# One layer of a hybrid attention and state-space encoder: Strassen products kept for keys, values, queries and gates only

## The chip, the cores and the metric

The kernel runs on one core of a Trainium2 chip. The time is the device time of one execution in microseconds (us). The engines are PE (TensorE: matrix products), DVE (VectorE), ACT (ScalarE), POOL (GpSimd) and SP (SyncE, which issues all the DMAs of this kernel). PEld is the weight load of PE. A product's small operand is called the weights here, the wide one the moving operand.

## The reference

One layer is computed for 2048 prompt frames and 32 sample frames, all in float32. `h` is the normed input, and one wide projection of `h` feeds every branch:

```python
h = RMSNorm_pre(x)                               # (L, 1024)
q, k, v, g_att, z, xbc, dt_raw, gate_a, gate_s = split(h @ w_in)   # 9760 columns
att = window_attention(rope(q), rope(k), v, sinks)                 # 16 heads, 4 of keys
branch_a = (att * silu(g_att)) @ w_attn_o
xs, B, C = split(silu(causal_conv4(xbc)))                          # 2048 + 512 + 512 columns
y = chunked_scan(xs, softplus(dt_raw + dt_bias), B, C) + d_skip * xs   # 32 heads, state 128
branch_s = group_rms_norm(y * silu(z)) @ w_ssm_o
out = (sigmoid(gate_a) * branch_a + sigmoid(gate_s) * branch_s) @ w_out
x = x + RMSNorm_post(out)
```

The outputs are `x` of both groups of frames, the newest keys and values, the conv tails and the final scan states.

## The kernel before

**Blocks and stages.** The prompt is cut into four blocks of 512 frames (blocks 0 to 3, `b` in the code). Block 1 also carries the 32 sample frames, so it has 544 columns. Everything is kept transposed: features on partitions, frames as columns. A block runs through three stages. In the *scan stage* it projects x, B, C and z and runs the chunked scan of four groups beside these products; the first three output products of the scan branch (`ssm_out`, 24 jobs for groups 0 to 2) are in it too. In the *attention stage* it projects keys, values, queries and attention gates, then the merge gates GS and GA; attention runs beside the first of these, and the eight `ssm_out` jobs of group 3 as well. In the *merge stage* it computes the attention output product (`ao`) and the last product (`ou`), beside which the next block's `h` is prepared (`stage_a`).

**Precision.** An operand `x` is split into a high part rounded to fp32r and the remainder, and a product takes three matmuls of such parts (`group`, line 178: 4 contraction tiles by 3 combinations, 12 matmuls). `h` stands in SBUF as `h1` (features 0 to 511) and `h2` (512 to 1023), each with both parts.

**Jobs and weights.** The program is a list of jobs in order (`jobs`). A projection job is a *pair* of 128 output columns. Each needs a list of weight entries of 128 partitions by 512 values; an entry with both parts is 512 KB. An entry is either computed from the raw weights (`alloc`: load 256 KB into `raw`, ACT rounds it at line 142, DVE subtracts at line 143) or loaded as ready parts from DRAM (line 131, `w<-wd`). Where `keep` is set, the computed parts are written to DRAM (line 147, `wd<-w`) for the later blocks. There are nine `w` buffers and four `raw` buffers; `supply` runs eight entries ahead of PE.

**Two ways to compute a pair.** `emit_both` takes the four plain entries a11, a12, a21, a22 and computes the two output tiles one after the other: 48 matmuls of 512 columns. ACT copies each tile out of PSUM (line 247). `emit_pair` computes the same pair by a Strassen step with seven products of half the columns: 84 matmuls of 256 columns (272 in block 1), with weight entries a11, a12, s2, s1, s3, s4, a22 and moving operands b11, b21, t2, t1, t3, b22, t4 (sums of quarters of `h`, made once per block in `stage_a`: `sums_a`, `sums_b`, `sums_c`). Its results are put together by ACT (line 293) after product 0 and by DVE (lines 295, 297, 299, 300) after products 2, 4 and 6; both write into the job's output tile. A Strassen pair uses two PSUM tiles of two banks each, out of two in the pool, so each is awaited again within a pair.

In block 0 every pair is computed by `emit_both`. While that goes on, POOL forms the four weight sums s1, s3, s2, s4 out of the raw entries (line 136), ACT and DVE split them, and five of the eight entries (a11 and the four sums) are written to DRAM. In blocks 1 to 3 every pair is a Strassen pair: 38 of them per block, 20 in the scan stage (8 of x, 4 of B and C, 8 of z) and 18 in the attention stage. Entries a12 and a22 are not all in DRAM: block 1 computes both from raw weights (and writes a12), blocks 2 and 3 load a12 and compute a22.

**What orders the work.** Beside the products, the steps of the scan, the attention and the norms are handed out one at each `tick`: twice per pair and once for every two entries of the other jobs. A scheduler then fixes the order on each engine, and moves matmuls of the next job in front of ones that must wait. Each engine then runs its instructions in that order. SP waits in order too: a DMA whose data or buffer isn't ready holds up those behind it. The small products of the scan (lines 627 to 670: chunk transposes, state and output products) stand in PE's order between the matmuls of line 178. The other lines that the prediction names are L680, where DVE updates the scan state H, L714, where POOL sums squares for the group norm, L1090, where ACT copies the `ou` product out (24 matmuls of 512 columns per job), and L121, the raw load.

## Time and profile before

| what | value |
|---|---|
| device time, three runs | 3401.42 us median (3390.09 to 3412.6) |
| device time of the profiled execution | 3400.23 us |
| its span, first to last instruction | 3398.4 us |
| granted TensorE clock, mean | 0.947 of full speed |
| PE busy | 3010.3 us (89%) |
| PE weight loads busy | 2636.6 us (78%) |
| DVE, ACT, POOL busy | 2283.3 (67%), 1315.1 (39%), 742.0 us (22%) |
| DMA moved | 827.30 MB, mean 243 GB/s |

Busy times are unions over the whole span and hide that the stages differ. Matmuls are pipelined, so their listed durations overlap and a busy PE isn't PE at its peak. The granted clock has two levels, 2.4 GHz (1.0) and 1.2 GHz (0.5); a mean of 0.88 in a stretch says that 24% of it ran at the lower one. The stages end and begin, in us from the span's start: block 0 scan 25 to 545, attention 545 to 885, merge to 1000; block 1 scan 1000 to 1440, attention to 1740, merge to 1855; block 2 scan 1855 to 2253, attention to 2528, merge to 2630; block 3 scan 2630 to 3024, attention to 3296, merge to the end.

### The profile page before, as it was taken

What the parts mean: (1) busy time and instruction counts of PE and PEld (TensorE: products, weight loads), DVE (VectorE), ACT (ScalarE), POOL (GpSimd) and SP (SyncE); (2) the same over time, 40 slices, a digit from 0 to 9 for tenths busy, and PEclk for the clock granted to TensorE, in tenths of its full rate; (3) what the DMA queues carried; (4) which work ended last, traced back from release to release, by engine and by line L of the source; (5) the groups of instructions that cost most, each with busy time, mean ns of one, the idle gap of its engine ahead of it and who ended that gap; (6) DMA issues with size and microseconds to landing.
All of it is one profiled execution on the core that took longest, in us unless ns stands there. A gap on an engine that the chain in (4) does not pass through costs nothing.

```text
span 3398.4 us, 55609 instructions
## 1 busy us (share of the span) xinstructions
PE 3010.3 (89%) x20263; PEld 2636.6 (78%) x20263; DVE 2283.3 (67%) x4427; ACT 1315.1 (39%) x3064; POOL 742.0 (22%) x778
## 2 busy tenths in 40 slices
PE   6878787888898889989999878999999988999998
PEld 5656566656688788988899777888888877888897
DVE  7887977677478868666635766766634877765732
ACT  5555544455344434224413433322413434322411
POOL 2554534233202322110010222120000222210000
PEclk9888888999999999999999988999999998999999
DMA  6667676737888878785786887886686887887684
GB/s 206 225 221 242 210 230 231 248 138 244 288 302 287 267 233 270 224 289 170 227 276 218 281 257 235 284 278 218 200 308 211 289 277 235 274 278 232 191 310 132
DMA packets 511993, 827.30 MB, mean 243 GB/s; under 512 B 38792, under 2 KB 334056, under 8 KB 511720
## 3 DMA queue, kind: packets, MB, share of 16 engines
q1 hardware_dynamic: 511720, 823.75, 73.5%
q8 instruction: 161, 2.64, 0.3%
q14 instruction: 112, 0.92, 0.1%
HBM read 638.50 MB, written 185.12 MB: 242 GB/s over the span
## 4 chain that ended last, share of the span: by engine, by line
PE 54%; DVE 16%; DMA 11%; POOL 6%; issue 6%; ACT 4%; SPq 2%; POOLq 0%; DVEq 0%; ACTq 0%
PE mm L178 45%; POOL raw L136 4%; DVE w L143 3%; DMA rr<-cd 3%; DMA raw<-in_w_in_dram 2%; DMA w<-wd 2%; PE sd L940 1%; DVE u L559 1%; PE sd L983 1%; DMA s<-zd 1%; PE sd L662 1%; PE sd L666 1%; SPq L121 1%; ACT rr L635 1%; DMA s<-rd 1%
## 5 line engine op out<-in xcount | busy, mean ns | idle before, releaser
L178 PE MATMUL mm<-h,w 128*128 128x256 f32 (+2 forms) x7432 | 1308.5, 328 | 206.0 <-ACT w L142 66.7
L178 PEld LDWEIGHTS mm<-h,w 128*128 128x128 f32 x7432 | 1102.1, 197 | 359.3 <-ACT w L142 77.2
L178 PE MATMUL mm<-t,w 128*128 128x256 f32 (+1 forms) x4104 | 574.2, 289 | 2.4 <-DMA w<-wd 2.4
L143 DVE TENSOR_TENSOR w<-raw,w 128x512 fp32r<-128x512 f32 x520 | 441.9, 861 | 160.5 <-ACT w L142 150.2
L178 PEld LDWEIGHTS mm<-t,w 128*128 128x128 f32 x4104 | 534.1, 193 | 8.2 <-issue 4.8
L178 PE MATMUL mm<-v,w 128*128 128x512 f32 (+1 forms) x2400 | 495.4, 360 | 26.6 <-ACT w L142 10.3
L142 ACT ACTIVATE w<-raw 128x512 fp32r<-128x512 f32 x520 | 321.2, 629 | 475.7 <-PE mm L178 203.1
L178 PEld LDWEIGHTS mm<-v,w 128*128 128x128 f32 x2400 | 397.3, 192 | 99.8 <-ACT w L142 12.3
L136 POOL TENSOR_TENSOR raw<-raw 128x512 f32<-128x512 f32 x152 | 228.8, 1505 | 295.0 <-DVE w L143 256.5
L635 ACT ACTIVATE rr<-rr,ncum 128x128 f32<-128x128 f32 (+1 forms) x544 | 167.9, 384 | 110.8 <-POOL rr L632 110.5
L299 DVE TENSOR_TENSOR xq<-mm,xq 128x512 f32<-128x512 f32 (+1 forms) x99 | 69.5, 702 | 167.9 <-PE mm L178 167.7
L178 PE MATMUL mm<-tA,w 128*128 128x512 f32 (+2 forms) x688 | 174.4, 341 | 0.0
L559 DVE SCALAR_TENSOR_TENSOR u<-xq,par,u 128x512 f32<-128x512 f32 x192 | 155.5, 831 | 11.0 <-ACT u L550 8.9
L821 POOL TENSOR_TENSOR s<-s,cs 128x512 f32<-128x512 f32 (+1 forms) x40 | 62.9, 1582 | 438.7 <-DVE s L819 313.5
L921 ACT ACTIVATE pt<-sd,nm 128x192 f32<-128x192 f32 (+3 forms) x260 | 105.0, 413 | 134.3 <-DVE nm L915 131.4
L632 POOL TENSOR_SCALAR_AFFINE_SELECT rr<-rr 128x1024 f32<-128x1024 f32 (+1 forms) x68 | 83.5, 1228 | 259.4 <-DMA rr<-cd 199.3
L178 PEld LDWEIGHTS mm<-tA,w 128*128 128x128 f32 x688 | 118.3, 188 | 13.7 <-ACT v L1090 0.2
L297 DVE TENSOR_TENSOR xq<-mm,xq 128x512 f32<-128x512 f32 (+1 forms) x99 | 69.3, 700 | 75.2 <-PE mm L178 74.4
L295 DVE TENSOR_TENSOR xq<-mm,xq 128x512 f32<-128x512 f32 (+1 forms) x99 | 69.0, 697 | 73.4 <-PE mm L178 72.9
L178 PE MATMUL mm<-S,w 128*128 128x512 f32 (+2 forms) x344 | 115.8, 337 | 0.1
L646 POOL TENSOR_TENSOR s<-xd,te 128x512 f32<-128x512 f32 (+1 forms) x68 | 75.8, 1117 | 172.2 <-DVE xd L643 171.2
L651 POOL TENSOR_TENSOR xl<-s,xh 128x512 fp32r<-128x512 f32 (+1 forms) x68 | 94.5, 1392 | 76.0 <-ACT xh L650 76.0
(272 smaller groups left out, 3990.6 us busy)
## 6 DMA issues: line engine op xcount, KB each, us to landing
w<-wd SPq DMA_DIRECT2D x838, 512.0 KB
wd<-w SPq DMA_DIRECT2D x292, 512.0 KB
raw<-in_w_in_dram SPq DMA_DIRECT2D x306, 256.0 KB
rr<-cd SPq DMA_DIRECT2D x64, 512.0 KB
ee<-cd SPq DMA_DIRECT2D x128, 128.0 KB
x<-in_x_prompt_dram SPq DMA_DIRECT2D x24, 512.0 KB
zd<-xq SPq DMA_DIRECT2D x48, 256.0 KB
s<-zd SPq DMA_DIRECT2D x48, 256.0 KB
```

Source lines behind the costliest of these rows:

```text
L136: pl.tensor_tensor(*(rawtiles[en["raw0"] + i] for i in (dst, x, y)), op=op)
L142: act.activation(w[:, 0], r, AF.Copy)
L143: vec.tensor_tensor(w[:, 1], r, w[:, 0].bitcast(F32), op=ALU.subtract)
L178: last_mm[0] = pe.matmul(ps, a[:, k, :], r(k, n0, n), start=start and k == 0 and i == 0, stop=stop and k == HK - 1 and i == len(ops) - 1)
L297: vec.tensor_tensor(two(y1), m57, twice(y0[:, n:]), op=ALU.add)
L299: vec.tensor_tensor(mid, m34, two(y1), op=ALU.add)
L559: vec.scalar_tensor_tensor(o[:, d0:d0 + n], src[:, t:t + n], convw[:, t, ci:ci + 1], o[:, d0:d0 + n], op0=ALU.mult, op1=ALU.add)
L632: pl.affine_select(w[:q, :, :q], w[:q, :, :q], pattern=[[0, 8], [1, q]], compare_op=ALU.is_ge, fill=-1e30, base=0, channel_multiplier=-1)
L635: act.activation(w[:q, h, :q], w[:q, h, :q], AF.Exp, scale=1.0, bias=ncum[:q, co + g * 8 + h:co + g * 8 + h + 1])
L646: pl.tensor_tensor(xe[:q].rearrange("p (h d) -> p h d", h=8), xd[:q], te[:q, hs].unsqueeze(2).broadcast_to([q, 8, 64]), op=ALU.mult)
L651: pl.tensor_tensor(xl[:q], xe[:q], xh[:q].bitcast(F32), op=ALU.subtract)
L921: act.activation(dst, src, AF.Exp, bias=nm[:, i:i + 1], scale=0.125, accum_out=den[:, i:i + 1])
```

## The change

**Which pairs are Strassen pairs.** `add_pair` gets a flag `fast`, set for keys, values, queries, attention gates, GS and GA (18 pairs per block). The 20 pairs of the scan stage are now computed by `emit_both` in blocks 1 to 3 too, with 48 matmuls of 512 columns (96 of 272 columns in block 1).

**Weights.** In block 0 the 20 plain pairs form no sums and write their four plain entries to DRAM; the 18 fast ones write seven entries (a11, a12, a22 and the four sums). Blocks 1 to 3 compute no entry: four loads for a plain pair, seven for a fast one.

**PSUM in `emit_both`.** For up to 512 columns both output tiles of a pair now share one PSUM tile of two banks; before, each had a tile of its own. In block 1 each has its own tile, split into two banks. ACT still copies each tile out.

**Quarters of `h`.** `h1` and `h2` now hold all four quarters b11, b12, b21, b22 through the scan stage, which the plain products need. t1, which lives where b12 does, is computed in four pieces in `sums_b`, written to DRAM (`t1d`), and brought back by `fetch_t1`, two DMAs put ahead of the last eight `ssm_out` jobs of the scan stage. The job for dt uses the plain form in all blocks (`emit_dt` goes).

```diff
--- before.py
+++ after.py
@@ emit_both @@
         flat, width, off = jb["dest"]()
+        tb = jb["tb"]
+        ts = [banks()] if tb <= 512 else [banks(), banks()]
         for i in range(2):
             if i:
                 between()
-            t = banks()[:, 0]
+            res = [(ts[0][:, i], 0, tb)] if tb <= 512 else [(ts[i][:, x, :n], n0, n) for x, (n0, n) in enumerate(split_n(tb))]
 
             def run():
-                for h, e in enumerate(jb["entries"][2 * i:2 * i + 2]):
...
-                    yield from group(t, e, m, 0, BT, h == 0, h == 1)
-            spread(run(), 6 * HK)
+                for ps, n0, n in res:
+                    for h, e in enumerate(jb["entries"][2 * i:2 * i + 2]):
...
+                        yield from group(ps, e, m, n0, n, h == 0, h == 1)
+            spread(run(), 6 * HK * len(res))
             used(2)
-            y = flat[:, off + i * width:off + i * width + BT]
-            act.copy(y, t)
+            y = flat[:, off + i * width:off + i * width + tb]
+            for ps, n0, n in res:
+                act.copy(y[:, n0:n0 + n], ps)
             jb["evac"][i](y)
@@ add_pair @@
-    def add_pair(b, view, c1, c2, tb, dest, evacs, **kw):
+    def add_pair(b, view, c1, c2, tb, dest, evacs, fast, **kw):
         a11, a12, a21, a22 = ((view, k0, c) for c in (c1, c2) for k0 in (0, HK))
+        kind = "pair" if b and fast else "both"
         if b == 0:
...
-                entries.append(dict(kind="plain", key=(c1, "a11"), load=False, keep=i == 0, raw=r0 + i, free=0))
+                entries.append(dict(kind="plain", key=(c1, name), load=False, keep=not fast or i != 2, raw=r0 + i,
+                                    free=0 if fast else 1))
 
             for name, dst, x, y, op, free in (("s1", 3, 2, 3, ALU.add, 0), ("s3", 2, 0, 2, ALU.subtract, 0),
-                                              ("s2", 0, 3, 0, ALU.subtract, 0), ("s4", 1, 1, 0, ALU.subtract, 4)):
+                                              ("s2", 0, 3, 0, ALU.subtract, 0), ("s4", 1, 1, 0, ALU.subtract, 4)) if fast else ():
...
-            kind = "both"
         else:
-            load = dict(a11=True, a12=b > 1, a22=False)
-            es = [raw_entry((c1, n), u, load.get(n, True), n == "a12" and b == 1)
-                  for n, u in (("a11", a11), ("a12", a12), ("s2", None), ("s1", None), ("s3", None), ("s4", None), ("a22", a22))]
-            kind = "pair"
+            names = ("a11", "a12", "s2", "s1", "s3", "s4", "a22") if fast else ("a11", "a12", "a21", "a22")
+            es = [raw_entry((c1, n), None, True, False) for n in names]
@@ stage_a @@
             def sums_a():
-                parts("b11", "b11")
+                for n in ("b11", "b12", "b22", "b21"):
+                    parts(n, n)
+
+            def sums_b():
+                nh = tb // 2
                 to("b11", "b12", "b11")
                 to("b12", "b22", "b12")
-                parts("t1", "b11")
-
-            def sums_b():
-                parts("b22", "b22")
-                parts("b21", "b21")
                 to("b22", "b22", "b11")
-                parts("t3", "b12")
+                st["t1d"] = dram.tile([P, 2, HK, HN], F32, name="t1d")
+                for k in range(HK):
+                    t = s2.tile([P, 2, HN], F32R, name="s2")
+                    act.activation(t[:, 0, :nh], raw("b11")[:, k], AF.Copy)
+                    vec.tensor_tensor(t[:, 1, :nh], raw("b11")[:, k], t[:, 0, :nh].bitcast(F32), op=ALU.subtract)
+                    dma(st["t1d"][:, :, k, :nh], t[:, :, :nh].bitcast(F32))
 
             def sums_c():
                 to("b21", "b21", "b22")
+                parts("t3", "b12")
@@ the job list @@
+        def fetch_t1(bk=bk, n=tb // 2):
+            for s_ in range(2):
+                dma(operand("t1", n)[:, s_].bitcast(F32), bk["st"]["t1d"][:, s_, :, :n])
...
         ssm_out(2)
+        if b:
+            jobs[-8]["pre"].append(fetch_t1)
...
-            (emit_dt if j else emit_plain)(j)
+            emit_plain(j)
```

**On PE, scan stage of block 3.** Before, the second pair of x and the first product of the third pair: `mm` are PSUM tiles, `h1`, `h2`, `t2` to `t4` the moving operands, `w` the weight buffers; after each row stands what it waits for (Activation and DVE: those engines, DMAHW: a DMA).

```order
L178 MATMUL mm_26637<-h1_99,w_26380 128x256 x2
L178 MATMUL mm_26637<-h2_100,w_26455 128x256 [waits DMAHW7_49,Activation_49]
L178 MATMUL mm_26637<-h2_100,w_26455 128x256 x11
L178 MATMUL mm_26637<-t2_101,w_26479 128x256 [waits DMAHW0_49]
L178 MATMUL mm_26637<-t2_101,w_26479 128x256 x11
L178 MATMUL mm_26638<-h1_99,w_26493 128x256 [waits DMAHW1_49,DVE_49,PE_49]
L178 MATMUL mm_26638<-h1_99,w_26493 128x256 x11
L178 MATMUL mm_26638<-t3_102,w_26545 128x256 [waits DMAHW4_49]
L178 MATMUL mm_26638<-t3_102,w_26545 128x256 x11
L178 MATMUL mm_26766<-h1_99,w_26598 128x256 [waits DMAHW7_49,DVE_49]
L178 MATMUL mm_26766<-h1_99,w_26598 128x256 x11
L178 MATMUL mm_26638<-h2_100,w_26559 128x256 [waits DMAHW5_49,DVE_49]
```

The same stage of the changed program, the third pair and the first product of the fourth:

```order
L178 MATMUL mm_24919<-h1_99,w_24642 128x512 [waits DMAHW4_49]
L178 MATMUL mm_24919<-h1_99,w_24642 128x512 x11
L178 MATMUL mm_24919<-h2_100,w_24644 128x512 [waits DMAHW5_49]
L178 MATMUL mm_24919<-h2_100,w_24644 128x512 x11
L178 MATMUL mm_24999<-h1_99,w_24806 128x512 [waits DMAHW2_49,Activation_49]
L178 MATMUL mm_24999<-h1_99,w_24806 128x512 x3
L178 MATMUL mm_24919<-h1_99,w_24720 128x512 [waits DMAHW0_49,Activation_49]
L178 MATMUL mm_24919<-h1_99,w_24720 128x512 x11
L178 MATMUL mm_24919<-h2_100,w_24722 128x512 [waits DMAHW1_49]
L178 MATMUL mm_24919<-h2_100,w_24722 128x512 x11
L178 MATMUL mm_24999<-h1_99,w_24806 128x512 x8
L178 MATMUL mm_24999<-h2_100,w_24808 128x512 [waits DMAHW3_49]
```

Before, the tile `mm_26637` waits for ACT after its first product (`h1_99`, then `h2_100`) and the second tile `mm_26638` for DVE ahead of its third; the next pair's `mm_26766` is begun early, and waits for DVE. Now one tile, `mm_24919`, takes both halves of a pair, and the second half (`w_24720`) waits for ACT; three or four matmuls of the next pair's tile `mm_24999` stand ahead of it.

**On SP, scan stage of block 0.** Before (`wd<-w`: ready parts to DRAM; `raw`: raw weights; `zd`: the z gate to DRAM):

```order
L147 DMA wd30_718<-w_714 128x1024
L147 DMA wd31_724<-w_720 128x1024
L147 DMA wd32_730<-w_726 128x1024
L147 DMA wd33_736<-w_732 128x1024
L121 DMA raw_738<-in_w_in_dram 128x4x128
L121 DMA raw_740<-in_w_in_dram 128x4x128
L121 DMA raw_742<-in_w_in_dram 128x4x128
L121 DMA raw_744<-in_w_in_dram 128x4x128
L577 DMA zd_795<-xq_757 128x512
L147 DMA wd34_786<-w_783 128x1024
L577 DMA zd_795<-xq_757 128x512
L147 DMA wd38_865<-w_861 128x1024
```

And now, at the same group's z pairs:

```order
L147 DMA wd18_639<-w_636 128x1024
L121 DMA raw_641<-in_w_in_dram 128x4x128
L147 DMA wd19_646<-w_643 128x1024
L121 DMA raw_648<-in_w_in_dram 128x4x128
L147 DMA wd20_688<-w_685 128x1024
L121 DMA raw_690<-in_w_in_dram 128x4x128
L147 DMA wd21_695<-w_692 128x1024
L121 DMA raw_697<-in_w_in_dram 128x4x128
L147 DMA wd22_739<-w_736 128x1024
L121 DMA raw_741<-in_w_in_dram 128x4x128
L147 DMA wd23_746<-w_743 128x1024
L121 DMA raw_748<-in_w_in_dram 128x4x128
```

Before, four raw loads follow a run of four writes, the last of which waits for the pair's last sum. Now each write is followed by one raw load, four entries ahead.

## Rows read from the trace of the kernel before

**Rows 1.** windows of the stages: us; then each engine's busy us (instructions), PEclk, DMA share, GB/s

```profile
25.00:545.00 520.00, 415.98 (x1898) 324.61 (x1896) 425.98 (x603) 257.84 (x516) 230.76 (x195) 0.88 0.68 227
545.00:885.00 340.00, 284.60 (x1368) 208.51 (x1368) 240.67 (x453) 173.82 (x408) 120.58 (x84) 0.92 0.60 210
1000.00:1440.00 440.00, 383.97 (x2987) 364.50 (x2986) 339.14 (x687) 172.70 (x404) 115.54 (x188) 0.94 0.81 259
1740.00:1855.00 115.00, 114.72 (x923) 114.14 (x922) 45.81 (x113) 31.70 (x64) 11.16 (x10) 1.00 0.65 213
1855.00:2253.00 398.00, 346.54 (x2519) 316.82 (x2518) 293.04 (x552) 146.59 (x331) 84.76 (x108) 0.94 0.82 266
2494.60:2527.00 32.40, 31.22 (x248) 30.20 (x249) 8.81 (x14) 5.25 (x11) 0.19 (x1) 1.00 0.92 325
2630.00:3024.00 394.00, 351.39 (x2540) 319.78 (x2539) 294.67 (x541) 146.58 (x332) 83.29 (x106) 0.95 0.81 269
900.00:950.00 50.00, 50.00 (x226) 40.61 (x225) 27.30 (x59) 20.10 (x37) 12.37 (x10) 1.00 0.97 321
```

**Rows 2.** waits of PE, scan stage of block 0: us in total, times, longest

```profile
PE mm L178 <- ACT w L142: 39.4, 13, 6.8
PE sd L662 <- DVE H L680: 19.5, 6, 6.4
PE sd L733 <- POOL s L714: 15.1, 3, 7.3
PE mm L178 <- DVE w L143: 9.3, 9, 2.3
```

**Rows 3.** waits of PE, scan stage of block 1

```profile
PE mm L178 <- DVE xq L295: 20.1, 4, 12.0
PE mm L178 <- DVE xq L299: 18.7, 15, 3.8
```

**Rows 4.** waits of PE, scan stage of block 2

```profile
PE mm L178 <- ACT xq L293: 11.8, 6, 6.9
PE mm L178 <- DVE xq L295: 10.7, 5, 8.7
...
PE mm L178 <- DVE xq L297: 4.9, 5, 2.4
PE mm L178 <- DMA w<-wd: 3.7, 3, 1.6
```

**Rows 5.** waits of PE, scan stage of block 3

```profile
PE mm L178 <- DVE xq L297: 7.0, 5, 5.3
...
PE mm L178 <- ACT xq L293: 5.2, 6, 2.2
PE mm L178 <- DVE xq L295: 4.4, 4, 1.9
```

**Rows 6.** groups by line, whole span: count, busy us, mean ns, idle before

```profile
L143 DVE TENSOR_TENSOR w<-raw,w 128x512 fp32r<-128x512 f32 x520 | 441.9, 861 | 160.5 <-ACT w L142 150.2 <-PE mm L178 2.5 <-DMA raw<-in_w_in_dram 0.6
```

**Rows 7.** timeline of evacuations, quiet stretches of block 2: start us, us, instruction

```profile
2505.37 0.42 DVE L300 TENSOR_TENSOR xq<-mm,xq 128x256 f32<-128x256 f32 x1
2516.21 0.42 DVE L300 TENSOR_TENSOR xq<-mm,xq 128x256 f32<-128x256 f32 x1
...
2612.08 0.59 ACT L1090 COPY v<-mm 128x512 f32<-128x512 f32 x1 [4.93 <-PE mm L178]
2617.60 0.59 ACT L1090 COPY v<-mm 128x512 f32<-128x512 f32 x1 [4.93 <-PE mm L178]
```

**Rows 8.** timeline of PE in the same quiet stretch

```profile
2496.28 1.57 PE L178 MATMUL mm<-t,w 128*128 128x256 f32 x12
2497.69 1.59 PE L178 MATMUL mm<-h,w 128*128 128x256 f32 x12
```

**Rows 9.** timeline of POOL and DVE, attention stage of block 0

```profile
828.82 6.04 POOL L136 TENSOR_TENSOR raw<-raw 128x512 f32<-128x512 f32 x4 [11.84 <-DVE w L143]
...
830.79 1.22 DVE L143 TENSOR_TENSOR w<-raw,w 128x512 fp32r<-128x512 f32 x1 [2.10 <-ACT w L142]
...
835.57 0.69 DVE L143 TENSOR_TENSOR w<-raw,w 128x512 fp32r<-128x512 f32 x1
```

More of the change, by code (lines that the diff above doesn't have):

```diff
@@ L1247, in qjobs @@
             c = C_Q + kv * 256
[L1248 removed]
+            pair(c, c + P, bk["stage_dest"], [bk["evac_q"](kv, a) for a in range(2)], name=("q", b, kv), fast=True)
         def gjobs(kv, **kw):
             c = C_G + kv * 256
[L1252 removed]
+            pair(c, c + P, bk["g_dest"](kv, ph), [bk["silu2"]] * 2, name=("g", b, kv), fast=True, **kw)
             if kv >= 2:
```

33 lines of the change are left out of this document (9 added, 24 removed).

## The prediction

> **What bounds the kernel now.** I read the windows of the stages first, because the change touches the three kinds of stage differently. In a quiet stretch of the gates GS and GA (2494.6 to 2527) PE is busy 31.2 of 32.4 us at full clock [rows 1]: PE is the bound. The scan stages are different. There PE is idle 104, 56, 51.5 and 42.6 us in blocks 0 to 3 (window less PE's busy time), and the granted clock is 0.88, 0.94, 0.94 and 0.95 [rows 1], so 24%, 12%, 12% and 10% of the time ran at 1.2 GHz. Then I read PE's waits in each scan stage, to see who ends the idle time. In block 0 it is mostly the weights: 39.4 + 9.3 = 48.7 us until a split entry is there (lines 142, 143), and 34.6 us of the scan's own waits for DVE and POOL [rows 2]. In blocks 1 to 3 the largest waits are for the evacuations of Strassen pairs: 38.8 us in block 1 [rows 3], 27.4 us in block 2 [rows 4], 16.6 us in block 3 [rows 5]. DVE, which makes most of these evacuations, is busy 82%, 77%, 74% and 75% of the four scan stages (426 of 520, and so on) [rows 1]. So the scan stages are bound by PE and DVE together: each waits for the other in turn.
>
> **What a pair costs on PE.** In the quiet stretch a Strassen pair ends every 10.84 us, and two `ou` jobs, which have the 48 matmuls of 512 columns of a plain pair, take 2 x 5.52 = 11.04 us [rows 7]. Seven products alone would take 7 x 1.41 = 9.9 us [rows 8]; the other 0.9 us of a quiet Strassen pair are its own waits. So the Strassen step saves 1.1 us of PE work per pair and gives 0.9 us back in its waits even where nothing else runs. For block 1 a matmul of 272 columns takes 115 / 923 = 0.125 us [rows 1], so a plain pair there is 96 x 0.125 = 12.0 us against 84 x 0.125 = 10.5 us: 1.5 us more.
>
> **Block 0, scan stage: -100 us.** Removed: for 20 pairs four sums on POOL, four splits each on ACT and DVE, and one write of 512 KB per pair. A split costs DVE 0.861 us on average [rows 6], so DVE loses 80 x 0.861 = 69 of its 426 us. PE's matmuls stay the same. What goes: the 48.7 us of waits for weights, since eight entries ahead are now two pairs instead of one and a raw load no longer waits for the pair's sums; about half of the 34.6 us of scan waits, because DVE and POOL have room, 17 us; and clock: at block 2's 0.94 the stage would run about 50 us at the lower level instead of 125, and with PE 80% busy that gives back 75 x 0.8 / 2 = 30 us. Sum 96. A second way: block 2's scan stage does the same scan beside the same pairs in 398 us; add about 20 us for DVE's remaining 104 splits and it is near 415, 105 us less than 520. I take 100. The bounds are 49 (only the weight waits) and 135 (down to 385 us, PE's 416 busy us less the 30 of the clock).
> The remaining splits should also get shorter. While POOL forms sums, a split takes 1.22 us on DVE, and 0.69 us when POOL has ended [rows 9]. The Trainium skill, "SBUF — State Buffer", section "SBUF: two separate sides", says that VectorE with two SBUF inputs and GpSimd take a shared port pair in turn, each for a whole instruction. The trace agrees, by that difference. By that rule the 104 splits left would cost 0.69 instead of 0.861 us, 18 us less of DVE's time; I don't add it to the sum, since PE waits for DVE only at times.
>
> **Block 0, attention stage: +8 us.** The work of 18 fast pairs stays, with two more writes each: 36 x 512 KB = 18.9 MB on top of 210 GB/s x 340 us = 71 MB [rows 1], which makes 266 GB/s, under the 321 GB/s that the windows show elsewhere. They are issued while POOL forms sums and few transfers are under way. Also the second half of each pair now waits for the ACT copy of the first with nothing in between. Bounds: nothing, and 36 x 1.63 = 59 us if every write at 321 GB/s stood in the path.
>
> **Block 1, scan stage: -20 us.** Twenty pairs at 1.5 us more PE work add 30 us. The evacuation waits of 38.8 us go: each half has its own PSUM tile, and before that tile is used again a whole half (6 us) runs. Their share of the lower clock goes too: of 12% of 440 us, 53 us, I take half, 26 us, which at PE's 87% gives 11 us. Sum 30 - 39 - 11 = -20. Bounds: +30 if the waits only change place, -40 if the clock goes up fully.
>
> **Blocks 2 and 3, scan stages: -3 and +7 us.** The pairs add 20 x 1.1 = 22 us each. The waits of 27.4 and 16.6 us go, and clock worth 5 us in each. A new wait comes: the second half of a plain pair needs the tile whose first half ACT is still reading. Three or four matmuls of the next pair stand in front, about 0.9 us, where the copy takes 0.59 us (like L1090 [rows 7]). Behind a waiting half stand all of PE's later products and the scan's. If ACT is on time this costs nothing; Strassen's own wait for ACT cost 11.8 us in block 2 [rows 4] with a like cover, so I take 8 us per block. Sums: 22 - 27 + 8 - 5 = -2, written as -3 with the conversions that no longer hold up loads, and 22 - 17 + 8 - 5 = +8, written as +7 for the same reason. Bounds from -30 (no waits left at all) to +21 in each.
>
> **Everything else: +1 us.** Blocks 1 to 3 compute no weights: 152 splits go, and their raw loads on SP's queue. PE's waits for loaded weights, 3.7 us in block 2 [rows 4], should fall by some 5 us in all. Against it, a fast pair now loads 7 x 524 = 3670 KB in 10.84 us, 339 GB/s, where the quiet stretch moves 325 GB/s at a DMA share of 0.92 [rows 1]. If 339 couldn't be had, the pair would take 11.3 us (3670 KB at 325 GB/s), 0.45 us more for some 42 pairs outside the attention steps: 19 us. I take 6, since at 0.92 of the engines there is room. Parking t1 adds per block four small splits, four writes and two reads: in the merge stage ACT idles 4.93 us per `ou` job [rows 7], and the reads have eight `ssm_out` jobs of 2.8 us (half an `ou` job) before the first fast pair. The reads wait on SP for the last z pair's matmuls, as the weight loads behind them do anyway. Cost nothing; if it weren't covered, some 3 us per block.
>
> **Sum.** -100 + 8 - 20 - 3 + 7 + 1 = -107 on the profiled execution's 3400.2 us (span 3398.4 and 1.8 around it), 3293 us. That execution lies 1.2 us under the median of the runs, 3401.4, so I predict 3293 us.
>
> **Rivals.**
> *The waits were all that held the scan stages (3201 us).* Block 0 gains its 135; blocks 1 to 3 lose all idle time and pay the pairs: 30 - 56, 22 - 51.5, 22 - 42.6. With +8 and +6 elsewhere: -213 + 14 = -199, and 3201. For it: DVE loses its splits and all evacuations of the scan stages in blocks 1 to 3. Against it: part of the idle time belongs to the scan's chain, which stays.
> *The copy wait takes Strassen's place (3397 us).* If each of the 60 plain pairs of blocks 0, 2 and 3 waits 2.0 us for ACT (11.8 us in 6 waits [rows 4]), that is 120 us, of which 16 are counted: +104 on the forecast, 3397, about no change. For it: ACT takes its instructions in order, and the scan's exponentials wait there for other engines. Against it: ACT is busy only 37% in block 2. The Trainium skill, "TensorE: Matmul & The Clock Gate", table at its head, says that ScalarE's queue is strictly first in, first out; one Strassen wait for ACT lasted 6.9 us [rows 4], ten times a copy, which agrees.
> *The scan's chain sets the pace (3438 us, slower).* Place: the small scan products in PE's order in blocks 1 to 3. If they wait as long for DVE, POOL and DMAs as before, a removed evacuation wait comes back there, and only the work counts: +30 + 22 + 22. Block 0 then gains only its 48.7, and the +8 and +6 stay: +39. It decides when less than 40 us of all relief beyond the weight waits comes. Against it: the evacuation waits are the largest single waits in blocks 1 to 3.
> *DMA binds (3357 us).* The 59 us of writes in block 0's attention stage and 19 us of loads, less the 14 counted: +64, and 3357. For it: the share of 0.92 in the quiet stretch. Against it: 0.97 and 321 GB/s were borne in block 0's merge stage with PE busy throughout [rows 1].
> *It doesn't do what it says.* The changed order shows 288 splits, all in block 0, and 72 sums: it does.
>
> **How the numbers follow.** Chances: the forecast 0.66, all waits gone 0.12, the copy wait 0.09, the chain 0.05, DMA 0.08. The forecast's own range is 3215 to 3355. The range that holds the time 8 times in 10 reaches from 3210 into the DMA case and short of the copy wait: 3210 to 3365. A measurement of this kernel can tell about 1%, 34 us, from no change. Faster by more than that: forecast, all waits gone and DMA, 0.86. Within it: the copy wait, 0.09. Slower: the chain, 0.05.
>
> **What would show it.** Right: block 0's scan stage near 420 us, with hardly a wait of PE for lines 142 and 143 and a clock of 0.93 or more; block 1's near 420 without waits for DVE on the pairs; blocks 2 and 3 within 10 us of before, with PE waiting for the pair's ACT copy some 8 us in each; the quiet fast pairs at 10.8 to 11.0 us; block 0's attention stage at 340 to 360 us. Wrong: block 0's scan stage above 470, or scan stages of blocks 1 to 3 longer than before.

## The result, and the profile after

The changed kernel takes 3210.7 us (median of four runs, 3203.3 to 3226.0) beside 3396.5 us for the kernel before (median of four too): a ratio of 0.945, 95% interval 0.940 to 0.950. That is 186 us faster. The profiled execution is the slowest of the four (3226.0 us, span 3224.2), so the stages below show 174 us of it. Measured again beside the runs below, the changed kernel took 3220.2 us, ratio 0.949 (0.946 to 0.952).

The gain by stage, from marks that both kernels have: the start of a block's first `s<-mm,dtb`, the end of its first `kr<-mm` (scan stage), the end of its last `tA<-xq` (attention stage), the next block's first mark (merge stage).

| us | scan 0 | attention 0 | merge 0 | scan 1 | attention 1 | scan 2 | attention 2 | scan 3 | attention 3 |
|---|---|---|---|---|---|---|---|---|---|
| before | 510.7 | 346.2 | 105.1 | 450.6 | 299.3 | 409.1 | 274.0 | 403.5 | 271.1 |
| after | 381.5 | 373.6 | 98.3 | 423.8 | 301.3 | 388.4 | 270.3 | 388.7 | 271.2 |
| difference | -129 | +27 | -7 | -27 | +2 | -21 | -4 | -15 | 0 |

The merge stages of blocks 1 to 3 differ by 1 us or less. Each stage is read from one profiled execution. Between executions of the changed kernel and its near copies below, a stage that is the same in both differs by up to 7 us.

From the page of the changed kernel, the engines' busy times and the clock by slices, and the lines of the splits and sums:

```profile
PE 3009.6 (93%) x19007; PEld 2570.8 (80%) x19007; DVE 1935.7 (60%) x3965; ACT 1227.0 (38%) x2942; POOL 617.3 (19%) x698
...
PEclk9999988898999999999999999999999999999999
...
L143 DVE TENSOR_TENSOR w<-raw,w 128x512 fp32r<-128x512 f32 x288 | 238.0, 841 | 96.6 <-ACT w L142 91.9
...
L136 POOL TENSOR_TENSOR raw<-raw 128x512 f32<-128x512 f32 x72 | 104.3, 1448 | 199.7 <-DVE w L143 195.6
```

PE is busy as long as before (3010 us), in a shorter span: the plain pairs of blocks 1 to 3 stream more columns, at a higher mean clock (0.973 of full speed, 0.947 before). The splits fell from 520 to 288 [rows 6], as the changed order showed. The clock is at 9 nearly throughout; the weak slices lie in block 0's attention stage.

The windows of the changed stages: scan 0, attention 0, scan 1, scan 2, scan 3 (columns as in [rows 1]):

```profile
29.00:410.00 381.00, 366.08 (x1868) 292.31 (x1866) 310.31 (x519) 206.24 (x435) 104.75 (x114) 0.99 0.86 283
411.00:784.00 373.00, 304.23 (x1382) 222.87 (x1380) 231.60 (x450) 168.31 (x405) 118.64 (x84) 0.89 0.66 238
883.00:1306.00 423.00, 405.53 (x3300) 391.39 (x3299) 276.27 (x591) 173.27 (x438) 109.72 (x186) 0.98 0.68 206
1711.00:2099.00 388.00, 367.14 (x1886) 295.75 (x1884) 244.06 (x478) 155.66 (x344) 86.56 (x106) 0.98 0.70 215
2463.00:2851.00 388.00, 367.62 (x1891) 295.77 (x1890) 241.47 (x462) 156.07 (x342) 88.06 (x105) 0.98 0.69 213
```

Where PE was idle 104, 56, 51.5 and 42.6 us in the four scan stages [rows 1], it is now idle 15, 17, 21 and 20 us, and the clock rose to 0.98 or 0.99 in each. Only block 0's attention stage went the other way: 69 us idle at a clock of 0.89, where [rows 1] show 55 us at 0.92.

PE's waits (us in total, times, longest) in scan 0; this answers to [rows 2]:

```profile
PE sd L726 <- POOL s L707: 6.5, 3, 2.2
PE mm L178 <- ACT xq L251: 2.8, 3, 1.3
...
PE sd L655 <- DVE H L673: 0.9, 2, 0.6
```

No wait for a weight is left, and the scan's own two largest waits fell from 19.5 + 15.1 to 0.9 + 6.5 us. The view of the kernel before goes on below the four lines of [rows 2] with five more waits of the scan, 17.9 us in all, among them:

```profile
PE sd L631 <- DVE ee L673: 8.7, 2, 4.4
PE sd L631 <- DVE rr L652: 5.1, 1, 5.1
```

So the scan's own waits were 52.5 us, not 34.6. In attention 0 of the changed kernel:

```profile
PE mm L178 <- ACT xq L251: 27.2, 10, 5.5
PE mm L178 <- ACT w L142: 18.1, 12, 2.3
PE mm L178 <- DVE w L143: 5.4, 2, 2.7
```

In scan 1 PE waits 0.5 us for a pair's evacuation instead of 38.8 [rows 3]. In scan 2, then in scan 3, the largest wait is the new one for the ACT copy, where [rows 4, 5] show waits for Strassen's evacuations:

```profile
PE mm L178 <- ACT xq L251: 15.6, 8, 3.9
...
PE mm L178 <- ACT xq L251: 9.2, 6, 2.6
```

A quiet Strassen pair still ends every 10.8 us, as in [rows 7] (10.84):

```profile
2335.84 0.42 DVE L289 TENSOR_TENSOR xq<-mm,xq 128x256 f32<-128x256 f32 x1
2346.63 0.43 DVE L289 TENSOR_TENSOR xq<-mm,xq 128x256 f32<-128x256 f32 x1
```

It now loads seven operands in that time, 3670 KB, or 340 GB/s, without a loss. The trace agrees: from 2325 to 2369 the DMAs moved 341 GB/s at a share of 0.95.

### The profile page after: what moved, and what is told of

Read it like the earlier page. It is cut to its first block, busy times and chain, and to the rows that moved or that the text cites. A ratio compares the mean times of both kernels' runs of the same rounds, so it can differ in the third digit from the quotient of the medians.

```text
span 3224.2 us, 51384 instructions
## 1 busy us (share of the span) xinstructions
PE 3009.6 (93%) x19007; PEld 2570.8 (80%) x19007; DVE 1935.7 (60%) x3965; ACT 1227.0 (38%) x2942; POOL 617.3 (19%) x698
## 4 chain that ended last, share of the span: by engine, by line
PE 61%; DVE 12%; DMA 10%; ACT 6%; POOL 5%; issue 5%; SPq 1%; DVEq 0%; POOLq 0%; ACTq 0%
PE mm L178 51%; DMA rr<-cd 4%; POOL raw L136 2%; ACT rr L628 2%; DVE u L552 2%; DVE w L143 2%; DMA raw<-in_w_in_dram 2%; PE sd L933 1%; PE sd L659 1%; POOL rr L625 1%; PE sd L976 1%; PE sd L655 1%; PE sd L959 1%; DMA s<-zd 1%; PE sd L663 1%
## 5 line engine op out<-in xcount | busy, mean ns | idle before, releaser
L178 PE MATMUL mm<-h,w 128*128 128x512 f32 (+2 forms) x8336 | 1602.4, 346 | 104.7 <-ACT xq L251 54.6
L178 PEld LDWEIGHTS mm<-h,w 128*128 128x128 f32 x8336 | 1317.3, 193 | 324.4 <-ACT xq L251 69.3
L143 DVE TENSOR_TENSOR w<-raw,w 128x512 fp32r<-128x512 f32 x288 | 238.0, 841 | 96.6 <-ACT w L142 91.9
L178 PE MATMUL mm<-t,w 128*128 128x256 f32 (+1 forms) x1944 | 271.2, 287 | 0.0
L178 PEld LDWEIGHTS mm<-t,w 128*128 128x128 f32 x1944 | 249.2, 190 | 4.4 <-issue 4.3
L142 ACT ACTIVATE w<-raw 128x512 fp32r<-128x512 f32 x288 | 174.6, 627 | 157.8 <-POOL raw L136 79.6
L628 ACT ACTIVATE rr<-rr,ncum 128x128 f32<-128x128 f32 (+1 forms) x544 | 168.7, 385 | 131.7 <-POOL rr L625 131.7
L251 ACT COPY xq<-mm 128x512 f32<-128x512 f32 (+1 forms) x226 | 110.9, 508 | 232.1 <-PE mm L178 231.8
L136 POOL TENSOR_TENSOR raw<-raw 128x512 f32<-128x512 f32 x72 | 104.3, 1448 | 199.7 <-DVE w L143 195.6
L906 DVE TENSOR_REDUCE mx<-sd 128x2 f32<-128x384 f32 (+3 forms) x140 | 66.0, 510 | 82.9 <-PE sd L933 78.2
L645 DVE SCALAR_TENSOR_TENSOR rr<-rr,sd 128x1024 f32<-128x1024 f32 (+1 forms) x68 | 79.3, 1165 | 53.0 <-ACT rr L628 53.0
```

Source lines behind the costliest of these rows:

```text
L136: pl.tensor_tensor(*(rawtiles[en["raw0"] + i] for i in (dst, x, y)), op=op)
L142: act.activation(w[:, 0], r, AF.Copy)
L143: vec.tensor_tensor(w[:, 1], r, w[:, 0].bitcast(F32), op=ALU.subtract)
L178: last_mm[0] = pe.matmul(ps, a[:, k, :], r(k, n0, n), start=start and k == 0 and i == 0, stop=stop and k == HK - 1 and i == len(ops) - 1)
L251: act.copy(y[:, n0:n0 + n], ps)
L628: act.activation(w[:q, h, :q], w[:q, h, :q], AF.Exp, scale=1.0, bias=ncum[:q, co + g * 8 + h:co + g * 8 + h + 1])
```

## The experiments

Three things were open: why block 0's attention stage lost 27 us, why scan 0 gained more than forecast, and which part of the change helped blocks 1 to 3. All stage lengths are between the marks above.

### Block 0's attention stage: own tile, or fewer writes

The second half of a plain pair waits for the copy of the first. The timeline of PE and ACT around one such wait in the changed kernel (start us, us, engine, line):

```profile
689.80 4.81 PE L178 MATMUL mm<-h,w 128*128 128x512 f32 x20
698.29 7.39 PE L178 MATMUL mm<-h,w 128*128 128x512 f32 x24 [3.69 <-ACT xq L251]
...
691.89 0.64 ACT L142 ACTIVATE w<-raw 128x512 fp32r<-128x512 f32 x1 [1.71 <-POOL raw L136]
693.26 0.63 ACT L142 ACTIVATE w<-raw 128x512 fp32r<-128x512 f32 x1 [0.74 <-POOL raw L136]
694.95 0.63 ACT L142 ACTIVATE w<-raw 128x512 fp32r<-128x512 f32 x1 [1.06 <-POOL raw L136]
696.62 0.63 ACT L142 ACTIVATE w<-raw 128x512 fp32r<-128x512 f32 x1 [1.04 <-POOL raw L136]
697.16 0.61 ACT L774 ACTIVATE xq<-xq 128x512 f32<-128x512 f32 x1
697.68 0.56 ACT L251 COPY xq<-mm 128x512 f32<-128x512 f32 x1
```

PE ends the first half at 694.61. The copy stands on ACT behind four splits of weight sums, each waiting about 1 us for POOL's next sum, and one short activation, and starts at 697.68. PE goes on at 698.29, right after the copy's end at 698.24. The copy itself is short; what is queued in front of it on ACT is long.

The Trainium skill, "Perfetto Trace Analysis", section "Matmuls", advises to rotate independent groups of matmuls through different PSUM banks, so that the evacuation of one overlaps the next. The two halves here do go to different 512-value slices of the tile, and yet the trace shows the wait. The next run takes it away by giving each half a tile of its own: in this program it goes with the tile, not with the slice.

**A tile for each half** (the edit in `emit_both`, up to 512 columns):

```diff
-        ts = [banks()] if tb <= 512 else [banks(), banks()]
+        ts = [] if tb <= 512 else [banks(), banks()]
...
-            res = [(ts[0][:, i], 0, tb)] if tb <= 512 else [(ts[i][:, x, :n], n0, n) for x, (n0, n) in enumerate(split_n(tb))]
+            res = [(banks()[:, 0, :tb], 0, tb)] if tb <= 512 else [(ts[i][:, x, :n], n0, n) for x, (n0, n) in enumerate(split_n(tb))]
```

> The changed kernel, but each half of a plain pair has its own PSUM tile in blocks 0, 2 and 3 too (they shared one), and nothing else differs. In the changed kernel PE waits for the ACT copy of a plain pair 26.5 us in block 0's attention stage, 15.6 us in block 2's scan stage and 9.2 us in block 3's. Theory A, the shared tile is what cost block 0's attention stage its 27 us: that stage falls from 374 to about 350 us between the markers (first K evacuation to the last product of the attention), the scan stages of blocks 2 and 3 by 5 to 15 us each, and the time goes from 3211 to about 3165 to 3185 us. Theory B, the attention stage is longer because of the two extra writes per fast pair and the sums on POOL: the copy waits vanish but PE waits for weights instead, the stage stays at 365 to 375 us, and the time is 3190 to 3215 us.

Measured: 3167.8 us, ratio 0.934 (0.932 to 0.936). Attention 0 falls to 332.5 us, by 41, more than theory A asked for; scan 2 falls by 16 and scan 3 by 3 us, where 5 to 15 were expected in each. Attention 0 in the window, and PE's largest waits there:

```profile
406.00:738.00 332.00, 285.63 (x1364) 211.58 (x1362) 236.24 (x450) 170.32 (x403) 116.38 (x82) 0.92 0.72 260
```

```profile
PE mm L178 <- ACT w L142: 23.8, 8, 5.5
PE sd L959 <- ACT pt L914: 8.3, 3, 5.5
```

The 27.2 us of copy waits are gone and the weight waits grew only from 18.1 to 23.8 us. PE's idle time fell by 22 us (69 to 46), and its busy time by 19 us (304 to 286) at a higher clock (0.89 to 0.92). Theory A holds: the shared tile cost this stage more than the 27 us. With own tiles the stage is 14 us shorter than before the change; PE waits 26.7 us for weights there, before it was 32.5 + 3.3 = 35.8. Why is not shown.

**Two operands less to write.** For the fast pairs a12 is made again in block 1 and a22 in blocks 1 to 3:

```diff
-                entries.append(dict(kind="plain", key=(c1, name), load=False, keep=not fast or i != 2, raw=r0 + i,
+                entries.append(dict(kind="plain", key=(c1, name), load=False, keep=not fast or i == 0, raw=r0 + i,
...
-            es = [raw_entry((c1, n), None, True, False) for n in names]
+            load = dict(a12=b > 1, a22=False) if fast else {}
+            es = [raw_entry((c1, n), dict(a12=a12, a22=a22).get(n), load.get(n, True), fast and n == "a12" and b == 1)
+                  for n in names]
```

> The changed kernel, but for the fast pairs a12 is made a second time in block 1 and a22 in blocks 1 to 3 from the raw weights, as in the kernel before; so block 0 writes five operands per fast pair instead of seven (less 18.9 MB), and blocks 1 to 3 convert 18 + 54 operands again. Theory A (the shared PSUM tile cost block 0's attention stage its 27 us): that stage falls by less than 8 us from 374, and the conversions in blocks 1 to 3 cost 0 to 15 us in all, so 3205 to 3225 us. Theory B (the extra writes cost it): the stage falls by 15 to 30 us to 345 to 360 us, and the time is 3185 to 3205 us.

Measured: 3217.1 us, ratio 0.948 (0.946 to 0.951). Attention 0 is 371.1 us, 2 us less, within the spread; the copy waits of PE there are 31.4 us. Theory B falls: the 36 writes cost this stage nothing that can be measured, and ready operands for these pairs gain nothing that can be measured on the whole.

### Is the Strassen step worth anything beside the attention

**All 38 pairs plain**, in all blocks; the weight sums, the input's sums and the parking of t1 are gone:

```diff
-            return steps + [[sums_a], [sums_b], [sums_c]]
+            return steps + [[sums_a]]
...
-        pair(C_K, C_K + P, bk["k_dest"], [bk["evac_k"](j) for j in range(2)], need=[f"s{b}.3"], fast=True,
+        pair(C_K, C_K + P, bk["k_dest"], [bk["evac_k"](j) for j in range(2)], need=[f"s{b}.3"],
...
```

> The changed kernel with plain products for all 38 pairs in every block: no Strassen step at all, so no sums on POOL for the weights, none of the input's sums, nothing parked; each weight written once and loaded ready. It asks what the Strassen step beside the attention is still worth. By the quiet rows a plain pair costs PE 0.2 us more than a fast one in blocks 0, 2 and 3 (11.04 against 10.84 us) and about 1.5 us more in block 1: 18 x (3 x 0.2 + 1.5) = 38 us more if only PE's work counts. Theory A (the sums on POOL and the weight waits set block 0's attention stage, with PE busy 293 of 361 us there): that stage falls from 374 by 40 to 70 us, and with the 38 us the time is 3170 to 3215 us. Theory B (the attention's own chain sets that stage): it falls by less than 15 us, and the time is 3230 to 3260 us.

> As the run with all 38 pairs plain, and each half of a pair with its own PSUM tile in blocks 0, 2 and 3. If the copy wait of the shared tile costs PE time (theory A of the first run), this is 30 to 60 us below the all-plain kernel with shared tiles, about 3130 to 3170 us, since all pairs gain. If the copy waits only stand where another wait would stand (theory B), the two agree within 15 us.

Measured: 3114.5 us, ratio 0.918 (0.916 to 0.920), with shared tiles, and 3082.3 us, ratio 0.909 (0.907 to 0.910), with a tile for each half. Both beat the changed kernel, by 3 and 4%. The first lies below even theory A's 3170: attention 0 fell by 104 us, to 269.2, where 40 to 70 were expected. The own tile took another 32 us, at the low end of what was expected (the time itself lies below the 3130 to 3170 us expected, since the kernel with shared tiles already did). Attention 0 gains only 3.5 us of them (269.2 to 265.7): without sums in ACT's queue the shared tile costs this stage almost nothing, with them it cost 41. Of the second kernel, PE's total from the page, and the windows of scan 0 and attention 0:

```profile
PE 2994.2 (97%) x17927; PEld 2515.1 (82%) x17927; DVE 1682.0 (55%) x3644; ACT 1220.0 (40%) x2939; POOL 506.9 (16%) x626
```

```profile
29.00:403.00 374.00, 360.69 (x1857) 290.28 (x1856) 304.69 (x518) 205.35 (x433) 93.03 (x108) 1.00 0.89 292
404.00:669.00 265.00, 264.20 (x1395) 202.59 (x1394) 159.42 (x389) 131.70 (x345) 20.21 (x18) 1.00 0.75 246
```

PE is busy 264.2 of 265 us in attention 0, at full clock. And the price expected for the plain pairs, 38 us, doesn't appear: attention 1, 2 and 3 take 294.3, 266.6 and 266.8 us beside 301.3, 270.3 and 271.2 with Strassen pairs. PE's whole busy time is lower (2994 against 3010 us, at a higher clock), though a plain pair streams 48 x 512 columns and a Strassen pair 84 x 256, an eighth less. In attention 1, 2 and 3 the step does save PE work: PE is busy 281.4, 258.9 and 259.4 us with Strassen pairs and 292.9, 266.0 and 266.2 us without. But PE is idle there 20.0, 11.3 and 11.8 us with them, and 1.5, 0.6 and 0.6 without. So the step saves 7 to 11 us per stage and its waits cost 11 to 19: no stage gets shorter by it. And in block 0 the sums for it cost 67 us more (332.5 against 265.7, own tiles both).

### Why scan 0 gained 129 us: the sums' load, or their chain

Two runs added to that fastest kernel what the sums load on the engines: 152 additions on POOL, then also a copy on ACT and a subtraction on DVE for each, over tiles that nobody else uses. The additions:

```diff
...
+        if en.get("junk"):
+            j = junk["t2"]
+            pl.tensor_tensor(j[1], j[0].bitcast(F32), j[0].bitcast(F32), op=ALU.add)
...
```

> The kernel with all 38 pairs plain and own tiles, plus, for each of the 152 weight operands of block 0, one addition on POOL of the size of a weight sum, over two tiles that nothing else touches: POOL's load of the kernel before, without anyone waiting for its result. It asks whether POOL's time for the sums alone (80 x 1.45 us in the scan stage, 72 x 1.45 in the attention stage) costs something, by the shared port or by the scan's own POOL work queued behind. Theory A (the load on POOL and DVE is what the sums cost): block 0's scan stage goes from 375 us up by 40 us or more and its attention stage from 258 us by 30 or more, splits on DVE get longer towards 0.86 us. Theory B (the chain costs it: a raw buffer comes free only after the sums, and the split of a sum waits for POOL): both stages grow by less than 15 us. Time by A 3150 us or more, by B 3080 to 3110 us.

> As the run with the 152 unread additions, plus for each of them one ACT copy and one DVE subtraction of the size of a split, also over tiles that nothing else touches: the whole engine load of the sums of the kernel before, on POOL, ACT and DVE, without its dependencies and its writes. DVE gets 80 x 0.8 = 64 us more in block 0's scan stage and 58 us more in its attention stage. Theory A (engine load): the scan stage goes from 375 us to above 450 (before: 511) and the attention stage from 258 to above 310 (with the sums: 332). Theory B (the chain of raw buffer, sum, split): the scan stage stays below 420 and the attention stage below 290.

Measured: 3193.9 us (scan 0 470.0 us, attention 0 265.8) and 3236.3 us (495.2 and 267.5). Without them attention 0 is 265.7 us, not 258. By the numbers theory A holds in scan 0 and theory B in attention 0, but the timeline of POOL forbids to read it so:

```profile
122.02 12.20 POOL L153 TENSOR_TENSOR t<-t 128x512 fp32r<-128x512 f32 x11
...
167.50 27.57 POOL L153 TENSOR_TENSOR t<-t 128x512 fp32r<-128x512 f32 x22
```

An instruction that waits for nothing was put early in its engine's order. All additions had run by 206 us (not 170, as the next expectation has it), in rows of up to 22, with the scan's POOL work behind them, and three single waits of PE (29.6, 22.6 and 19.4 us) make most of the loss. Attention 0 had none of the load. The runs say nothing on sums spread over the stages.

So the additions were made to read the raw buffer of each operand, which puts them where it lands (the last two lines in the second run alone):

```diff
...
+            v = r.rearrange("p (k c) -> p k c", k=2)
+            pl.tensor_tensor(j[0], v, v, op=ALU.add)
...
+            act.activation(j[1], j[0].bitcast(F32), AF.Copy)
+            vec.tensor_tensor(junk["t3"][0], j[0].bitcast(F32), j[1].bitcast(F32), op=ALU.subtract)
...
```

> The two runs before this left the question open: an addition that reads nothing of the program stands at the head of POOL's order, and all 152 ran in the first 170 us, in rows of up to 22, so their load wasn't that of the sums. Here the kernel with all 38 pairs plain and own tiles has, for each of the 152 weight operands of block 0, one addition on POOL of the size of a weight sum that reads the raw buffer of that operand, so that it stands where that buffer has landed; nobody reads its result, but the raw buffer comes free only after it. Theory A (POOL's and DVE's load from the sums set block 0's scan stage before): the scan stage goes from 375 us to above 420, with DVE's splits near 0.95 us as before. Theory B (the chain raw, sum, split, buffer free set it): it stays under 395 us. In the attention stage (266 us without sums, 332 with them and own tiles) the load is 72 additions of 1.45 us; A expects above 290 us, B under 275. Time by A 3140 us or more, by B 3080 to 3110 us.

> As the run with additions that read the raw buffers, plus an ACT copy and a DVE subtraction of each addition's result, over spare tiles that PE never reads: sums and splits of the kernel before with the order of that chain, but no PE product waits for them and they are not written. If the sums' whole engine load in its order is what cost block 0's scan stage 511 us (before) against 375, this stage goes above 470 us; if PE's waits for the pair's own weights (a lookahead of one pair) made it, it stays below 430 us. Attention stage: with the sums and own tiles it is 332 us; load alone would give above 310, the chain through PE and the writes below 290.

Measured: 3132.6 us, ratio 0.923 (0.921 to 0.925), and 3178.2 us, ratio 0.936 (0.934 to 0.938). Windows of scan 0 and attention 0, of the run with additions and then, in the second fence, of the one with splits too:

```profile
30.00:439.00 409.00, 372.45 (x1864) 298.93 (x1862) 348.36 (x520) 206.17 (x434) 199.32 (x194) 0.97 0.82 267
439.00:715.00 276.00, 268.84 (x1392) 205.22 (x1391) 186.05 (x389) 132.27 (x345) 93.26 (x79) 0.98 0.72 237
```

```profile
32.00:471.00 439.00, 381.08 (x1855) 302.32 (x1853) 407.89 (x604) 253.51 (x520) 222.27 (x195) 0.94 0.77 249
471.00:762.00 291.00, 276.41 (x1402) 209.77 (x1403) 224.38 (x452) 163.90 (x405) 96.94 (x78) 0.96 0.67 223
```

| us | no sums | + additions | + splits | sums that are used |
|---|---|---|---|---|
| scan 0 | 374.7 | 409.3 | 439.2 | 510.7 (before) |
| attention 0 | 265.7 | 276.4 | 290.8 | 332.5 (changed kernel, own tiles) |

Neither theory holds alone: in both runs both stages lie between the bounds set. In scan 0 the additions cost 35 us and the splits 30, in attention 0 11 and 14. PE's waits in scan 0 of the second run show how, the largest two and the only one for a weight:

```profile
PE sd L715 <- POOL s L696: 16.8, 3, 9.5
PE sd L644 <- DVE H L662: 11.5, 7, 3.9
...
PE mm L185 <- ACT w L143: 1.7, 1, 1.7
```

All waits other than for weights come to 55 us there, where they were 52.5 us in the kernel before and are 13 us without sums. So the load alone, on POOL, ACT and DVE, brings the scan's waits back in full. The last 72 us of scan 0 come only when the sums are part of the program; then PE waits 48.7 us for weights too [rows 2]. The window of the kernel before, between the marks:

```profile
29.00:539.00 510.00, 408.74 (x1868) 319.14 (x1867) 419.88 (x593) 254.04 (x509) 225.09 (x189) 0.88 0.69 228
```

Beside the second run that is 43 us more idle time (101 against 58), about the weight waits, and 28 us more busy time (409 against 381), at a clock of 0.88 instead of 0.94. Three things can make the weights late: raw buffers held through all four sums, a lookahead of one pair, one more entry to write per pair. How the waits divide among them wasn't tried. In attention 0 the last step is 42 us.

### Blocks 1 to 3: plain products, or ready operands

**Strassen with ready operands**: the kernel before, with all seven operands of each pair written in block 0.

```diff
-                entries.append(dict(kind="plain", key=(c1, "a11"), load=False, keep=i == 0, raw=r0 + i, free=0))
+                entries.append(dict(kind="plain", key=(c1, name), load=False, keep=i != 2, raw=r0 + i, free=0))
...
```

> The kernel before, with the Strassen step on all pairs and the sums for all pairs in block 0, but with all seven weight operands of every pair written in block 0 and loaded ready in blocks 1 to 3: nothing but the ready operands of the change. It separates the change's two parts in blocks 1 to 3, whose scan stages fell by 27, 21 and 15 us. Theory A, the plain products beside the scan gave that (no evacuations of Strassen pairs on DVE): here the three scan stages stay within 8 us of before (451, 409, 404 us), and PE still waits for DVE and ACT on the pairs there. Theory B, the removed conversions gave it (38 ACT copies and 38 DVE subtractions less per block after the first): the three stages fall by 40 us or more in all. Block 0 has 76 writes of 512 KB more; by the run that took back 36 writes (the same time, 3217 against 3211 us) that should cost under 15 us. Time by A 3385 to 3405 us, by B 3330 to 3360 us.

**Plain products without ready operands**: the changed kernel, whose plain pairs make a12 again in block 1 and a22 in blocks 1 to 3.

```diff
...
-            es = [raw_entry((c1, n), None, True, False) for n in names]
+            load = {} if fast else dict(a12=b > 1, a22=False)
+            es = [raw_entry((c1, n), dict(a12=a12, a22=a22).get(n), load.get(n, True), not fast and n == "a12" and b == 1)
+                  for n in names]
```

> The changed kernel, but the plain pairs beside the scan make two of their four operands again from the raw weights as the kernel before did (the second of the first half in block 1, the second of the second half in blocks 1 to 3): plain products without the ready operands. It is the complement of the Strassen run with ready operands, which shortened the three scan stages by 10, 17 and 4 us where the whole change shortened them by 27, 21 and 15. If the two parts add, the three stages here are 434, 405 and 393 us (the change's 424, 388 and 389 plus what the ready operands gave). If either part is enough, because both only make room on DVE, they stay within 6 us of the changed kernel's, 418 to 430, 382 to 394 and 383 to 395 us, and the time is 3205 to 3230 us.

| us | scan 1 | scan 2 | scan 3 | ratio to before |
|---|---|---|---|---|
| before | 450.6 | 409.1 | 403.5 | 1 |
| ready operands alone | 440.6 | 392.2 | 399.2 | 0.994 (0.992 to 0.997) |
| plain products alone | 436.9 | 387.4 | 388.9 | 0.956 (0.954 to 0.959) |
| both | 423.8 | 388.4 | 388.7 | 0.945 (0.940 to 0.950) |

The first run fits neither of its theories: 31 us in all, where A allowed 8 per stage and B asked for 40, and a time of 3378.6 us, between the two. Its 76 more writes go with a block 0 that is 19 us longer (scan 0 523.2 us, attention 0 352.5), where under 15 were expected. In scan 1 the two parts seem to add (10 + 14 = 24 of 27 us); with up to 7 us of spread in each stage this is weak. In scans 2 and 3 the plain products alone do all of it. With them PE waits less for DVE anyway, and the ready operands have nothing left to give that these runs show. The second run took 3242.9 us, 13 us above the upper end of what was expected. Its scan 0 is 388.8 us, 7 to 12 longer than in two executions of the changed kernel, although it writes less there; why stays open.

The changed kernel itself, run again beside these:

> The changed kernel again, on the chip of this group, so that the others can be held against it: 3200 to 3220 us, and block 0's attention stage at 370 to 376 us.

Measured: 3220.2 us, 0.2 over what was expected, attention 0 at 371.2 us; the other stages within 5 us of the table at the head.

## Why the prediction was right or wrong

The forecast was 3293 us, the time is 3210.7: the direction is right, and so are the waits that were to go, but the gain is 186 us instead of 107. The time lies 0.7 us inside the stated range (3210 to 3365) and below the forecast's own (3215 to 3355), and two of the four executions lie below both. That it is inside is luck: had block 0's attention stage lost the 8 us that were forecast and not 27, the time would be some 19 us less. What was wrong is the sentence "part of the idle time belongs to the scan's chain, which stays": of 104, 56, 51.5 and 42.6 us idle in the scan stages, 15 to 21 are left. The rival "The waits were all that held the scan stages", with a chance of 0.12, describes these stages better (3201 us; its terms add up to -211, not -213, so 3203). Term by term:

- **Block 0, scan stage: -100, measured -129.** The weight waits went, all 48.7 us, as forecast. Mis-sized were the two other parts. "About half of the 34.6 us of scan waits" was too little: the scan's waits were 52.5 us, and idle time fell by 89 us (104 to 15), so 40 of it besides the weights. And the clock went to 0.99, not 0.94: the lower level held 24% of 511 us before, 123 us, and 2% of 381 us now, 8 us. Those 115 us at PE's 80% give back 46 us instead of 30. 89 + 46 = 135, near the 129; between the marks PE lost 86 us of idle and 43 of busy time, which is 129. The runs with spread additions show why the scan's waits went too: they come from the load of sums and splits on POOL, ACT and DVE, which by itself makes 65 of the 136 us between scan 0 before and without sums. The "second way" came to 415 by rounding down: 398 + 20 is 418.
- **Block 0, attention stage: +8, measured +27.** The step that failed is the price of "the second half of each pair now waits for the ACT copy of the first with nothing in between", which was named there and given no number of its own; the writes, which were priced, cost nothing beyond the spread (2 us). Alone the shared tile costs 41 us in this stage, of which 14 came back in a way that no run explains. The copy shown is 0.56 us, but stands behind splits that wait for POOL.
- **Block 1, scan stage: -20, measured -27.** Right in mechanism and near in size: no wait for DVE on the pairs, clock 0.98. But by the runs some 10 us of it come from the ready operands, as far as the spread lets one say, which the term had at nothing here.
- **Blocks 2 and 3, scan stages: -3 and +7, measured -21 and -15.** The copy waits came as named: 15.6 and 9.2 us, where 8 each were taken. Mis-sized was "clock worth 5 us": in block 2 the lower level fell from 12% of 409 us, 49 us, to 4% of 388, 16 us, and 33 us less at nine tenths busy are 15 us. And PE's other idle time, which the term left as it was, went: besides the pairs' and the weights' waits of [rows 4] some 20 of the 51.5 us idle were left; besides the copy waits it is now 21 - 15.6 = 5. In block 3 PE's largest wait before was the scan's (`PE sd L733 <- POOL s L714: 10.3, 3, 5.3`, the line above those of [rows 5]), so that "the evacuation waits are the largest single waits in blocks 1 to 3" isn't true there.
- **Everything else: +1, measured -10** (-7 in merge 0, -4 in attention 2, +2 in attention 1, -1 in merge 1 and in merge 2). "If 339 couldn't be had": it could, 340 GB/s at 10.8 us per pair, and the run without the 36 writes gained 2 of the rival's 59 us in attention 0, within the spread; so the rival "DMA binds" falls.
- **The splits that remain** were to go from 0.86 towards 0.69 us. In scan 0 the mean is 0.82 us (88.1 us for 109; before 0.95), in attention 0 0.90. With no sums at all (all pairs plain) they are 0.83 and 0.70 us, and with spread additions 0.93 and 0.81. So additions on POOL beside them raise the mean by about 0.1 us. The splits beside the scan, where POOL has the scan's own work, are another 0.13 us longer; that POOL is the reason there too isn't shown by a run of its own. The Trainium skill, "SBUF — State Buffer", section "SBUF: two separate sides", has VectorE, with two SBUF inputs, and GpSimd take turns on a shared port pair for whole instructions; these means agree in direction, and the single splits at 0.69 and 1.22 us [rows 9] do too.

The chain rival ("The scan's chain sets the pace") is refuted: in block 0 the scan's waits went away with the load, and in blocks 1 to 3 the removed waits didn't come back in the scan's products. The copy-wait rival named the right new wait, but priced it where it is small (15.6 and 9.2 us); it is large where ACT's queue holds splits that wait for POOL: 41 us in attention 0 with the sums, 3.5 without.

## What to carry to other kernels

Price a removed load by the waits of everything that shares its engines, and the clock with it: here a stage whose PE went from 80% busy to 96% gained its idle time and half as much again. Before a product-saving scheme is refined, run the kernel without it: in the attention stages of blocks 1 to 3 the saved matmuls were given back in waits, and in block 0 the operand sums and what comes with them cost 136 us in the scan stage and 67 in the attention stage, 203 us. By the prediction's prices for a quiet pair, an estimate, the step for all pairs could save 38 x (1.1 + 1.1 + 1.5) = 141 us in blocks 1 to 3 if it never waited. A shared output tile makes the next product wait not for one copy, but for everything queued ahead of that copy.

## What the runs showed of the hardware that was not expected

How much of a wait's price is the clock. The same products of attention 0 kept PE busy 264 of 265 us at a granted clock of 1.00 with all pairs plain, 286 of 332 us at 0.92 with Strassen sums and own tiles, and 304 of 373 us at 0.89 in the changed kernel. From the first to the last the stage grew by 108 us: 68 us are idle time, and 40 us are the same work, part of it at 1.2 GHz: 0.89 is 22% of the stage, 82 us, at the lower of the two levels, and half of these 82 us is 41. In the stages with the lower clock PE waited for ACT again and again; with all pairs plain it hardly waited at all.

What an addition on POOL costs DVE. The run with the spread additions alone gave DVE nothing more to do, and yet DVE got slower: the 389 instructions of attention 0 kept it busy 186 us instead of 159, and those of scan 0 (520 and 518) 348 us instead of 305. ACT's busy time stayed (132.3 and 131.7 us in attention 0). POOL's grew by 73 and 106 us, so here each microsecond of added POOL work made DVE about 0.4 us busier. That is one way by which a load on POOL reaches the scan's work on DVE; the other is POOL's own queue, and no run parts the two.
